# Moving the norm factors' small matmuls and the scaling and convolution of the first results into the third unit's time

## The chip, the cores and the metric

The kernel runs on one core of a Trainium2 chip. The metric is the device time of one execution in microseconds (us). A profile adds the core's span from its first to its last instruction, which is a little shorter. TensorE (PE in the rows) does the matmuls, VectorE (DVE) and ScalarE (ACT) the elementwise work, GpSimd (POOL) a few tiny operations, and SyncE's queue (SP) issues nearly all DMAs.

## The reference

One layer of an encoder over a prompt of 1024 rows and a sample of 256 rows, of width 1024, in float32. What matters here is its first part:

```python
h = rms_norm(x, norms[i, 0])            # x * rsqrt(mean(x*x) + eps) * g
b, c, v = jnp.split(h @ w_in, 3, -1)    # w_in: 1024 x 3072
u = c * v
conv = sum(up[:, j:j+S] * conv_w[j] for j in range(3))   # up: u padded by a row at each end
mix = (b * conv) @ w_out
x = x + rms_norm(mix, norms[i, 1])
```

A gated feed-forward network of width 2816 with its own norms follows.

## The kernel before, in words

**Products.** A float32 product is made of three products of parts: each operand is split into a high part (ScalarE's copy in a rounded type) and a low part (VectorE's subtraction), and `product` (L209) issues high x high, high x low and low x high for each 128 rows of the sum. The prompt's 1024 rows and 1024 features are cut in quarters `a11`, `a12`, `a21`, `a22`, and sums of quarters `s1` to `s4` save one of eight block products (a Strassen-like scheme): one unit of 256 output features takes seven prompt products of 12 matmuls with 512 columns, and two sample products of 24 matmuls with 256 columns. `Block` (L219) holds a unit's PSUM banks `x`, `y`, `z`, `sg`, `su`; its products go x(a11), y(a12), x(s2), z(s1), x(s3), the two sample products, x(a22), z(s4). Between them `x` is copied out by ScalarE, and VectorE adds `y` or `z` to the copy. `make` (L186) splits a unit's weights and forms their sums; `load` (L171) asks for a unit's weights with two DMAs.

**Units.** The 1024 features of each of c, v and b are done in four slices, in the order c, v, b of each slice (`SEQ`). `start` (L516) writes out the first three units by hand, without a scheduler (`manual_schedule`, L720): its order in the code is the order on each engine. The first unit is c, plain products with tiles `c__`, `csg`, `csu`; the second is v (`b = Block(uv, ...)`, PSUM tiles `xv`, `yv`, `zv`, `sgv`, `suv`); the third is b (`b3 = Block(ub, ...)`, L682, tiles `xp__676`, `yp__677`, `zp__678`, `sgp`, `sup`). From the fourth on (L746) a scheduler orders the same steps.

**The norm.** The products are made of x times g alone; the factor 1/rms of each row is applied afterwards, squared, to c times v (`rows_c.end()`, L685 multiplies c's results `row` by `r2`; then `u` = `row` times v). For it, ten row blocks of x are loaded (`load_row`, L476), squared and summed by ScalarE into `rt` (`square_row`, L480). Two of them are in flight; each square frees the place that the next load waits for. `norm_of` (L487) turns four (or two) sums into factors: VectorE's scaling (L122), GpSimd's power (L123), VectorE's square into `rq`, and a split in `rh` (ScalarE) and `rl` (VectorE). `spread` (L497) brings them to all partitions with eight (or four) small matmuls against an identity (`bc`, L503), and ScalarE squares that into `r2` (L508, L510). There are three groups: rows 0 to 3, rows 4 to 7, and the sample's 8 and 9.

**The order around the change.** In the second unit the small matmuls stand before x(s2) (L650), before x(s3) (L666) and before z(s4) (L676). In the third unit VectorE scales, multiplies and convolves (`conv`, L414) c and v after x(a11) (L685 to L700), and the fourth unit's weights are made; the load of the fifth unit's weights (`load(SEQ[4])`, L707) stands before the stores of the first result (`store`, L428, DMAs `zd<-zst`).

Of the kernel before, what the change touches and what calls it, by code (L numbers as in the profile page):

```python
# [14 lines left out]
P = 128  # L15
# [21 lines left out]
def encoder_kernel(ctx: ExitStack, tc: tile.TileContext, xT, x, g0T, gB, cwT, w1, w2, w3, w4, out_p, out_s):  # L37
# [148 lines left out]
    def make(u, what):  # L186

        if u is None:
            return
        rw = raw[u]  # L190
        if what == "sums":
            sub(rw[:, 0], rw[:, 1], rw[:, 0])
            sub(rw[:, 1], rw[:, 2], rw[:, 1])
            sub(rw[:, 2], rw[:, 0], rw[:, 2])
            add(rw[:, 3], rw[:, 3], rw[:, 2])
            return
        blocks = {"g": slice(0, 4, 3), "u": slice(1, 3), "t13": slice(0, 2), "t24": slice(2, 4)}[what]
# [125 lines left out]
    class EvC:  # L323
# [33 lines left out]
    class EvMul:  # L357
# [27 lines left out]
        def add12(self, z):  # L385
            add(self.t["12"], self.t["12"], z)
            self.times(1, 0, self.t["12"])

        def read22(self, x, z, mult=True):
            copy(self.tmp("22"), x)  # L390
            add(self.t["22"], self.t["22"], z)
            if mult:
                self.times(1, 1, self.t["22"])

# [92 lines left out]
    def norm_of(c):  # L487

        t0, n = CH[c]
        i0, m = t0 // P, n // P  # L490
        rc = rt[:, i0 : i0 + m]
        rstd(rc, rc, m)
        mul(rq[:, i0 : i0 + m], rc, rc)
        norms[c] = [small(m, f"r{p}{c}", F32R) for p in "hl"]
        split(*norms[c], rc)
# [20 lines left out]
    def start():  # L516
# [85 lines left out]
        def scaled_add(out, src, f0, other, op=ALU.add):  # L602
            for k in range(KH):
                nc.vector.scalar_tensor_tensor(
                    out=out[:, k], in0=src[:, k], scalar=g0k(f0 + k), in1=other[:, k], op0=ALU.mult, op1=op
                )
# [26 lines left out]
        make(uv, "sums")  # L633
        b.run("x", "g", 0, "a11", True)
        b.run("y", "g", 1, "a12", True)
        make(uv, "t24")
        parts("s1", s1)
        put(s1)
        make(uv, "t13")
        ev.read11(b.bank["x"])  # L640
        ev.add11(b.bank["y"], mult=False)
        for i in range(2, 6):
            square_row(i)
            load_row(i + 2)
            if i == 3:
                norm_of(0)
        b.sample(evac=False)
        scaled_add(s3, xq["a22"], KH, s2)
        parts("s3", s3)
        spread(0, 5)  # L650
        b.run("x", "t24", 0, "s2", False)
        scaled_add(s4, xq["a12"], KH, s2)
        put(s2, s3)
        square_row(6)
        load_row(8)
        ev.read12(b.bank["x"])
        square_row(7)
        load_row(9)
        load(SEQ[3])
        parts("s4", s4)  # L660
        put(s4)
        b.run("z", "t13", 0, "s1", True)
        make(ub, "g")
        make(ub, "u")
        norm_of(1)
        spread(1, 6)  # L666
        b.run("x", "t13", 1, "s3", False)
        b.drop("t13")
        ev.read22(b.bank["x"], b.bank["z"], mult=False)
        for i in (8, 9):  # L670
            square_row(i)
        make(ub, "sums")
        norm_of(2)
        b.run("x", "t24", 1, "a22", False)
        b.drop("t24")
        spread(2, 7)  # L676
        make(ub, "t24")
        b.run("z", "u", 1, "s4", False)
        b.release_u()
        make(ub, "t13")  # L680
        ev3, un = EvMul(0, 0), SEQ[3]
        b3 = Block(ub, ev3)  # L682
        b3.run("x", "g", 0, "a11", True)
        ev3.read11(b3.bank["x"])
        rows_c.end()  # L685
        new_u(0)
        ev.times(0, 0, ev.t["11"])
        ev.times(0, 1, b.bank["x"])
        ev.times(1, 1, ev.t["22"])
        ev.sample(b.bank["sg"], b.bank["su"])  # L690
        ev.add12(b.bank["z"])
        b3.run("y", "g", 1, "a12", True)
        ev3.add11(b3.bank["y"], mult=False)
        make(un, "g")
        b3.run("x", "t24", 0, "s2", False)
        ev3.read12(b3.bank["x"])
        ev.conv(0)
        b3.run("z", "t13", 0, "s1", True)
        make(un, "u")
        ev.end()  # L700
        b3.run("x", "t13", 1, "s3", False)
        b3.drop("t13")
        ev3.times(0, 0, ev3.t["11"])
        make(un, "sums")
        ev3.read22(b3.bank["x"], b3.bank["z"])
        b3.sample(evac=False)
        load(SEQ[4])  # L707
        make(un, "t24")
        ev3.sample(b3.bank["sg"], b3.bank["su"])
        b3.run("x", "t24", 1, "a22", False)  # L710
        b3.drop("t24")
        make(un, "t13")
        ev3.read21(b3.bank["x"])
        b3.run("z", "u", 1, "s4", False)
        b3.release_u()
        ev3.add12(b3.bank["z"])
        ev3.end()

    turn[0] = 6
    with tc.manual_schedule():  # L720
        start()


    w2t, w2r = [], []
# [21 lines left out]
    for n in range(3, len(SEQ)):  # L746
        u = SEQ[n]
        follow = SEQ[n + 1 : n + 3] + [None, None]
        final = n == len(SEQ) - 1
        ev = EvC(u[2]) if u[1] == 1 else EvMul(u[1], u[2])  # L750
        if final:
            put(r2)
            w2_steps()
        b = Block(u, ev, *follow[:2], final)
        b.p12()
        b.p657()
        b.sample()
        if final:
            for i in ORDER2[:2]:
                load_z(i, 0, KD - 2)  # L760
        b.p43()
# [186 lines left out]
    class EvF:  # L948
# [33 lines left out]
        def copy22(self, x):  # L982
            self.c22 = self.tmp("c22")
            copy(self.c22, x)
# [610 lines left out]
```

## Time and profile before

| | us |
|---|---|
| median of 3 runs | 1273.38 (1272.29 to 1276.47) |
| the profiled execution | 1275.11 |
| its span | 1273.3 |
| TensorE busy | 1243.2 |
| VectorE busy | 835.0 |
| ScalarE busy | 464.7 |
| GpSimd busy | 24.0 |
| DMA, mean rate over the span | 163 GB/s |

Every engine works through its own instructions in order and waits at each for what it needs. "Busy" is the time in which instructions of the engine ran; TensorE's weight loads run beside its matmuls. A row of a timeline says when an instruction started, how long it took, the engine, the line, what it wrote and read, and in brackets how long the engine had been idle before it and what ended that. Times are counted from the span's start.

### The profile page before, as it was taken

The page shows a single profiled execution, that of the slowest core. Times are in us where ns is not written, and L with a number is a line of the kernel's source. Part 1 is how long each engine was busy: PE and PEld are TensorE (multiplying, and loading weights), DVE is VectorE, ACT ScalarE, POOL GpSimd, SP SyncE. Part 2 cuts the span into 40 slices and gives each one's busy share as a digit, 9 for nine tenths or more (in the row PEclk, how much of TensorE's full clock was granted, in tenths as well). Part 3 has the DMA queues.
Part 4 walks back from the last instruction along what each step waited for, and adds up shares of the span by engine and source line. Part 5 has one row for each costly group of instructions (what it writes and reads, how often), then busy time and mean ns, then how long its engine had stood idle before and what let it go on. Part 6 is the DMA issues. An engine that isn't in the chain of part 4 may idle for free.

```text
span 1273.3 us, 15950 instructions
## 1 busy us (share of the span) xinstructions
PE 1243.2 (98%) x6239; PEld 1057.2 (83%) x6239; DVE 835.0 (66%) x1157; ACT 464.7 (36%) x695; POOL 24.0 (2%) x49
## 2 busy tenths in 40 slices
PE   9699999999999989999999999999999999999997
PEld 7578888888878878888888888888888888888886
DVE  6857674666376587664755655655647479869566
ACT  7633332334143454343433433433434342212011
POOL 0000000000011100000000000000000000000000
PEclk9889999999999999999999999999999999999999
DMA  8403131233954303542532533524525888766794
GB/s 307 156 1 116 66 115 36 76 116 113 333 194 158 137 34 102 163 151 94 178 121 93 189 114 118 188 88 147 157 88 190 293 282 306 266 229 214 274 337 177
DMA packets 186124, 207.38 MB, mean 163 GB/s; under 512 B 8000, under 2 KB 146368, under 8 KB 185024
## 3 DMA queue, kind: packets, MB, share of 16 engines
q1 hardware_dynamic: 185616, 205.83, 48.3%
q8 instruction: 49, 0.80, 0.3%
q10 hardware_dynamic: 432, 0.53, 0.1%
q14 instruction: 27, 0.22, 0.0%
HBM read 134.89 MB, written 71.43 MB: 162 GB/s over the span
## 4 chain that ended last, share of the span: by engine, by line
PE 87%; DVE 4%; DMA 4%; ACT 3%; issue 1%; POOL 0%; SPq 0%; DVEq 0%; ACTq 0%; POOLq 0%
PE xo L1394 12%; PE zo L1394 6%; PE mx L810 5%; PE yo L1394 3%; DMA wrf__3033<-w 1%; PE xf__3501 L213 1%; PE xp__676 L213 1%; PE xf__3503 L213 1%; PE xf__4757 L213 1%; PE xf__4370 L213 1%; PE xf__7079 L213 1%; PE xf__6866 L213 1%; PE xf__6692 L213 1%; PE xf__6479 L213 1%; PE xf__6305 L213 1%
## 5 line engine op out<-in xcount | busy, mean ns | idle before, releaser
L810 PE MATMUL mx<-w2s,zs 128*128 128x512 f32 x480 | 111.2, 391 | 0.0
L810 PEld LDWEIGHTS mx<-w2s,zs 128*128 128x128 f32 x480 | 89.5, 188 | 18.2
L106 ACT ACTIVATE st<-act 128x640 fp32r<-128x640 f32 x77 | 56.8, 737 | 94.7 <-DMA actd<-st 64.0
L97 DVE TENSOR_TENSOR st<-act,st 128x640 fp32r<-128x640 f32 x77 | 63.2, 820 | 20.9 <-ACT st L106 20.4
L100 DVE TENSOR_TENSOR y<-y,xo 128x512 f32<-128x512 f32 x85 | 58.2, 685 | 27.4 <-PE xo L1394 27.1
L1394 PE MATMUL xo<-w4t,us 128*128 128x512 f32 x273 | 68.9, 389 | 0.0
L1394 PEld LDWEIGHTS xo<-w4t,us 128*128 128x128 f32 x273 | 51.3, 188 | 10.6
L1394 PE MATMUL xo<-w4t,ut 128*128 128x512 f32 x222 | 55.5, 390 | 0.0
L106 ACT ACTIVATE w4t<-w4r 128x1024 fp32r<-128x1024 f32 (+1 forms) x23 | 23.5, 1023 | 72.5 <-DVE w4r L97 59.6
L1394 PEld LDWEIGHTS xo<-w4t,ut 128*128 128x128 f32 x222 | 41.7, 188 | 8.7
L100 DVE TENSOR_TENSOR y<-y,zo 128x512 f32<-128x512 f32 x45 | 30.8, 685 | 17.3 <-PE zo L1394 17.0
L1394 PE MATMUL xo<-w4b,ut 128*128 128x512 f32 x165 | 41.6, 390 | 0.0
L1394 PE MATMUL zo<-w4t,ut 128*128 128x512 f32 x165 | 41.5, 389 | 0.0
L1394 PE MATMUL zo<-w4b,ut 128*128 128x512 f32 x165 | 41.5, 389 | 0.0
L1426 ACT ACTIVATE junk<-y 128x1024 f32<-128x1024 f32 (+1 forms) x12 | 11.0, 919 | 73.7 <-DVE y L100 72.4
L1394 PEld LDWEIGHTS xo<-w4b,ut 128*128 128x128 f32 x165 | 31.0, 188 | 6.6
L1394 PEld LDWEIGHTS zo<-w4t,ut 128*128 128x128 f32 x165 | 31.0, 188 | 6.5
L1394 PEld LDWEIGHTS zo<-w4b,ut 128*128 128x128 f32 x165 | 31.0, 188 | 6.4
L424 DVE SCALAR_TENSOR_TENSOR row<-u,cw,row 128x1024 f32<-128x1024 f32 (+1 forms) x32 | 27.7, 881 | 5.8 <-ACT row L422 5.6
L1394 PE MATMUL yo<-w4b,us 128*128 128x512 f32 x114 | 28.9, 389 | 0.0
L106 ACT ACTIVATE w4b<-w4r 128x512 fp32r<-128x512 f32 (+1 forms) x22 | 18.1, 839 | 28.3 <-DMA us<-actd 12.5
L97 DVE TENSOR_TENSOR w4t<-w4r,w4t 128x1024 fp32r<-128x1024 f32 (+1 forms) x23 | 26.9, 1172 | 0.8 <-ACT w4t L106 0.8
(2115 smaller groups left out, 3357.9 us busy)
## 6 DMA issues: line engine op xcount, KB each, us to landing
actd<-st SPq DMA_DIRECT2D x154, 320.0 KB, 2.9
ut<-actd SPq DMA_DIRECT2D x20, 1024.0 KB, 6.8
us<-actd SPq DMA_DIRECT2D x62, 256.0 KB, 5.0
ut<-actd SPq DMA_DIRECT2D x16, 768.0 KB, 8.8
zd<-zst SPq DMA_DIRECT2D x32, 320.0 KB, 3.1
zs<-zd SPq DMA_DIRECT2D x8, 1024.0 KB, 6.8
w4r<-w SPq DMA_DIRECT2D x11, 512.0 KB, 4.4
w4r<-w SPq DMA_DIRECT2D x22, 256.0 KB, 5.5
```

What stands on the lines that cost most here:

```text
L97: nc.vector.tensor_tensor(out=out, in0=a, in1=b, op=ALU.subtract)
L100: return nc.vector.tensor_tensor(out=out, in0=a, in1=b, op=ALU.add)
L106: nc.scalar.activation(out, a, AF.Copy)
L213: nc.tensor.matmul(out[:, :n], stat(w, k), mov(part, k), start=first and k == 0 and j == 0, stop=last and k == KH - 1 and j == 2, skip_gro ...
L424: nc.vector.scalar_tensor_tensor(out=out, in0=src, scalar=cw[:, j, dd : dd + 1], in1=out, op0=ALU.mult, op1=ALU.add)
L810: nc.tensor.matmul(mx[i][h], zs[i][:, part, k], w2t[k][:, w, h * H : (h + 1) * H], start=k == 0 and j == 0, stop=k == KD - 1 and j == 2,)
L1394: nc.tensor.matmul(acc, stat[n, c, j][:, ap], w[wp], start=starts and jn == 0 and m == 0, stop=jn == len(grp) - 1 and m == 2, skip_group_c ...
L1426: nc.scalar.activation(junk, src, AF.Square, accum_out=acc[:, col : col + 1])
```

## The change

`norm_of` is cut in two: the scaling and power stay, and the square and split become `parts_of_norm`. `read22` becomes `copy22` and `add22`. In `start`, the sums `s3` and `s4` are formed earlier, the squares of rows stand behind the copies of product results, the first group of small matmuls goes behind x(s2), the second and third into the third unit, and what the third unit does on VectorE is reordered. The third unit's PSUM banks are named one by one, and the fourth unit does its sample products earlier. The diff, without the helper lines:

```diff
         make(uv, "t24")
         parts("s1", s1)
         put(s1)
+        scaled_add(s3, xq["a22"], KH, s2)
         make(uv, "t13")
         ev.read11(b.bank["x"])
-        ev.add11(b.bank["y"], mult=False)
-        for i in range(2, 6):
-            square_row(i)
-            load_row(i + 2)
-            if i == 3:
-                norm_of(0)
+        next_row(2)
+        next_row(3)
+        norm_of(0)
         b.sample(evac=False)
-        scaled_add(s3, xq["a22"], KH, s2)
-        parts("s3", s3)
-        spread(0, 5)
-        b.run("x", "t24", 0, "s2", False)
+        high3, low3 = hi_lo("s3", s3)
+        high3(0)
+        high3(2)
+        low3()
         scaled_add(s4, xq["a12"], KH, s2)
         put(s2, s3)
-        square_row(6)
-        load_row(8)
+        next_row(4)
+        next_row(5)
+        parts_of_norm(0)
+        b.run("x", "t24", 0, "s2", False)
         ev.read12(b.bank["x"])
-        square_row(7)
-        load_row(9)
-        load(SEQ[3])
+        ev.add11(b.bank["y"], mult=False)
         parts("s4", s4)
         put(s4)
+        spread(0, 5)
         b.run("z", "t13", 0, "s1", True)
         make(ub, "g")
         make(ub, "u")
-        norm_of(1)
-        spread(1, 6)
         b.run("x", "t13", 1, "s3", False)
         b.drop("t13")
+        make(ub, "sums")
         ev.read22(b.bank["x"], b.bank["z"], mult=False)
-        for i in (8, 9):
-            square_row(i)
-        make(ub, "sums")
-        norm_of(2)
+        next_row(6)
+        next_row(7)
+        load(SEQ[3])
+        norm_of(1)
         b.run("x", "t24", 1, "a22", False)
         b.drop("t24")
-        spread(2, 7)
         make(ub, "t24")
+        parts_of_norm(1)
+        make(ub, "t13")
         b.run("z", "u", 1, "s4", False)
         b.release_u()
-        make(ub, "t13")
...
         b3.run("x", "g", 0, "a11", True)
         ev3.read11(b3.bank["x"])
+        square_row(8)
+        square_row(9)
+        norm_of(2)
+        make(un, "g")
+        b3.run("y", "g", 1, "a12", True)
+        ev3.add11(b3.bank["y"], mult=False)
+        spread(1, 1)
+        parts_of_norm(2)
+        b3.run("x", "t24", 0, "s2", False)
+        ev3.read12(b3.bank["x"])
+        spread(2, 5)
         rows_c.end()
...
+        b3.run("z", "t13", 0, "s1", True)
         ev.times(1, 1, ev.t["22"])
...
+        mul(samp(rows[0]), samp(rows[0]), by_halves(b3.bank["sg"]))
         ev3.read21(b3.bank["x"])
+        make(un, "sums")
+        ev3.add22(b3.bank["z"])
+        make(un, "t24")
         b3.run("z", "u", 1, "s4", False)
         b3.release_u()
...
         ev3.end()
+        make(un, "t13")
+        load(SEQ[4])
...
-        b.p657()
-        b.sample()
+        if n == 3:
+            b.nxt2 = None
+            b.sample()
+            b.p657()
+            load(follow[1])
+        else:
+            b.p657()
+            b.sample()
```

How this moves instructions, at three places. The first is ScalarE's list in the second unit, from the first two squares of rows that the norm's first group needs (`rows_392`, `rows_395`) on; `rh_466` and `rh_533` are the high parts of the first group's factors, before:

```order
L482 ACTIVATE rows_392,rt<-rows_392 128x1024
L482 ACTIVATE rows_395,rt<-rows_395 128x1024
L93 ACTIVATE rh_466<-rt 128x4
L482 ACTIVATE rows_458,rt<-rows_458 128x1024
L482 ACTIVATE rows_461,rt<-rows_461 128x1024
L106 ACTIVATE s3h<-xa_120 128x1024 x2
L508 ACTIVATE r_111<-bc_534 128x512
```

And on ScalarE at the same place after the change:

```order
L488 ACTIVATE rows_392,rt<-rows_392 128x1024
L488 ACTIVATE rows_395,rt<-rows_395 128x1024
L106 ACTIVATE s3h<-xa_120 128x1024 x2
L488 ACTIVATE rows_461,rt<-rows_461 128x1024
L488 ACTIVATE rows_464,rt<-rows_464 128x1024
L93 ACTIVATE rh_533<-rt 128x4
L106 ACTIVATE c__549<-xv__409 128x512
L106 ACTIVATE s4h<-xa_118 128x1024 x2
L519 ACTIVATE r_111<-bc_558 128x512
```

The copies of `s3` moved ahead, and the squares of rows 4 and 5 (`rows_461`, `rows_464`) now stand before the factors' high part.

VectorE's list at the same place, before (`rl_` is the factors' low part, `xa_120` becomes `s3`, `xa_118` becomes `s4`):

```order
L97 TENSOR_TENSOR s1l<-xa_119,s1h 128x1024 x2
L94 TENSOR_TENSOR wt13p__451<-wrp__144,wt13p__451 128x1024
L100 TENSOR_TENSOR c__454<-c__454,yv__410 128x512
L122 TENSOR_SCALAR rt<-rt 128x4
L103 TENSOR_TENSOR rq<-rt 128x4
L94 TENSOR_TENSOR rl_467<-rt,rh_466 128x4
L604 SCALAR_TENSOR_TENSOR xa_120<-xa_120,g_94,xa_117 128x512 x4
L97 TENSOR_TENSOR s3l<-xa_120,s3h 128x1024 x2
L604 SCALAR_TENSOR_TENSOR xa_118<-xa_118,g_94,xa_117 128x512 x4
```

VectorE's list there after the change:

```order
L97 TENSOR_TENSOR s1l<-xa_119,s1h 128x1024 x2
L615 SCALAR_TENSOR_TENSOR xa_120<-xa_120,g_94,xa_117 128x512 x4
L94 TENSOR_TENSOR wt13p__455<-wrp__144,wt13p__455 128x1024
L122 TENSOR_SCALAR rt<-rt 128x4
L97 TENSOR_TENSOR s3l<-xa_120,s3h 128x1024 x2
L615 SCALAR_TENSOR_TENSOR xa_118<-xa_118,g_94,xa_117 128x512 x4
L103 TENSOR_TENSOR rq<-rt 128x4
L94 TENSOR_TENSOR rl_534<-rt,rh_533 128x4
L100 TENSOR_TENSOR c__458<-c__458,yv__410 128x512
```

The forming and splitting of `s3` and the forming of `s4` now stand between the scaling of the sums (L122) and the factors' low part.

The second place is ScalarE's list around the second and the third group, before (`rh_598` and `rh_636` are the high parts of their factors, `bc_602` and `bc_652` what their small matmuls write, `c__624` the copy of x(s3), `wgp__589` to `wt13p__673` the third unit's weights):

```order
L93 ACTIVATE wup__592<-wrp__152 128x1024
L93 ACTIVATE rh_598<-rt 128x4
L508 ACTIVATE r_111<-bc_602 128x512
L106 ACTIVATE c__624<-xv__409 128x512
L482 ACTIVATE rows_561,rt<-rows_561 128x1024
L482 ACTIVATE rows_566,rt<-rows_566 128x1024
L93 ACTIVATE rh_636<-rt 128x2
L510 ACTIVATE r_111<-bc_652 128x2x128
L93 ACTIVATE wt24p__658<-wrp__152 128x1024
L93 ACTIVATE wt13p__673<-wrp__152 128x1024
```

ScalarE's list there after the change (`c__602` is the copy of x(s3), `c__665` and `c__714` are the third unit's first two copies, `wgp__671` is a fourth unit's weight):

```order
L106 ACTIVATE c__602<-xv__409 128x512
L488 ACTIVATE rows_527,rt<-rows_527 128x1024
L488 ACTIVATE rows_530,rt<-rows_530 128x1024
L93 ACTIVATE wt24p__628<-wrp__152 128x1024
L93 ACTIVATE rh_632<-rt 128x4
L93 ACTIVATE wt13p__636<-wrp__152 128x1024
L106 ACTIVATE c__665<-xb__651 128x512
L488 ACTIVATE rows_606,rt<-rows_606 128x1024
L488 ACTIVATE rows_609,rt<-rows_609 128x1024
L93 ACTIVATE wgp__671<-wrp__611 128x1024
L519 ACTIVATE r_111<-bc_687 128x512
L93 ACTIVATE rh_698<-rt 128x2
```

The copy of x(s3), which x(a22) waits for, now stands ahead of the second group, and the third group came behind the third unit's first copy. On TensorE the second group's small matmuls stand behind the third unit's y(a12) and the third group's behind its x(s2).

The third place is SyncE's queue in the third unit, before (`wrp__568` and `wrp__840` are the weights of the fourth and fifth unit, `zd<-zst` the stores of the first result):

```order
L478 DMA rows_566<-x 128x1024
L182 DMA wrp__568<-w 128x2x512
L184 DMA wrp__568<-w 128x1024
L182 DMA wrp__840<-w 128x2x512
L184 DMA wrp__840<-w 128x1024
L434 DMA zd<-zst_864 128x5x128 x2
L434 DMA zd<-zst_869 128x5x128 x2
L434 DMA zd<-zst_888 128x5x128 x2
L434 DMA zd<-zst_893 128x5x128 x2
```

SyncE's queue there after the change (`wrp__611` and `wrp__895` are the same two units' weights):

```order
L484 DMA rows_609<-x 128x1024
L182 DMA wrp__611<-w 128x2x512
L184 DMA wrp__611<-w 128x1024
L440 DMA zd<-zst_848 128x5x128 x2
L440 DMA zd<-zst_853 128x5x128 x2
L440 DMA zd<-zst_882 128x5x128 x2
L440 DMA zd<-zst_887 128x5x128 x2
L182 DMA wrp__895<-w 128x2x512
L184 DMA wrp__895<-w 128x1024
```

The fifth unit's weights moved behind the eight stores. From the fifth unit's first products on, each engine's list is as before.

## Rows read from the trace of the kernel before

**Rows 1.** Waits of TensorE: who waited for whom; total us, times, longest us.

```profile
PE bc L503 <- ACT rh L93: 13.4, 3, 9.9
```

**Rows 2.** Timeline of TensorE, 45 to 96 us: start us, us, what, idle before.

```profile
45.65 0.28 PE L213 MATMUL suv__412<-hsh,wup__386 128*128 128x256 f32 x1
47.86 0.33 PE L503 MATMUL bc<-ident_r,rh 128*128 128x128 f32 x1 [1.93 <-ACT rh L93]
...
48.89 0.45 PE L213 MATMUL xv__409<-s2h,wt24p__442 128*128 128x512 f32 x1
...
64.41 0.48 PE L503 MATMUL bc<-ident_r,rh 128*128 128x128 f32 x1 [9.85 <-ACT rh L93]
...
66.18 0.73 PE L213 MATMUL xv__409<-s3h,wt13p__451 128*128 128x512 f32 x1
...
72.04 0.50 PE L213 MATMUL xv__409<-a22h,wt24p__442 128*128 128x512 f32 x1 [0.69 <-ACT c__624 L106]
...
76.63 0.33 PE L503 MATMUL bc<-ident_r,rh 128*128 128x128 f32 x1 [1.59 <-ACT rh L93]
...
95.25 0.28 PE L213 MATMUL sgp__679<-hsh,wgp__589 128*128 128x256 f32 x1
```

**Rows 3.** Stretches: us, busy of each engine, granted clock, DMA share, GB/s.

```profile
57.26:70.91 13.65, 6.50 (x19) 5.51 (x20) 5.91 (x9) 4.69 (x6) 1.02 (x1) 0.50 0.41 149
77.74:81.15 3.41, 3.41 (x10) 2.64 (x9) 2.38 (x3) 1.95 (x3) 0.00 (x0) 0.50 0.00 0
```

**Rows 4.** The chain that ended last, 66 to 88 us: start us, us, what.

```profile
66.39 4.99 PE xv__409 L213 x12
...
77.38 4.39 PE zv__413 L213 x12
...
84.53 2.72 PE yp__677 L213 x12
```

**Rows 5.** Timeline of ScalarE, 45 to 52 us.

```profile
45.12 1.04 ACT L482 ACTIVATE rows<-rows 128x1024 f32<-128x1024 f32 x1
...
48.86 1.06 ACT L482 ACTIVATE rows<-rows 128x1024 f32<-128x1024 f32 x1 [1.05 <-DMA rows<-x]
...
50.91 1.06 ACT L482 ACTIVATE rows<-rows 128x1024 f32<-128x1024 f32 x1 [0.90 <-DMA rows<-x]
```

**Rows 6.** Timeline of VectorE, 42 to 104 us.

```profile
42.03 2.35 DVE L97 TENSOR_TENSOR s1l<-xa,s1h 128x1024 fp32r<-128x1024 f32 x2
44.30 1.22 DVE L94 TENSOR_TENSOR wt13p__451<-wrp__144,wt13p__451 128x1024 fp32r<-128x1024 f32 x1
...
47.92 2.73 DVE L604 SCALAR_TENSOR_TENSOR xa<-xa,g,xa 128x512 f32<-128x512 f32 x4
...
81.05 2.88 DVE L103 TENSOR_TENSOR row<-row,r 128x1280 f32<-128x1280 f32 x2
...
91.67 3.27 DVE L424 SCALAR_TENSOR_TENSOR row<-u,cw,row 128x1024 f32<-128x1024 f32 x4 [2.09 <-ACT row L422]
...
102.56 0.68 DVE L100 TENSOR_TENSOR c__788<-c__788,zp__678 128x512 f32<-128x512 f32 x1
```

**Rows 7.** Timeline of GpSimd: its power operations.

```profile
46.54 1.03 POOL L123 TENSOR_TENSOR rt<-rt,nhalf 128x4 f32<-128x4 f32 x1 [45.24 <-DVE rt L122]
...
455.17 0.54 POOL L123 TENSOR_TENSOR n_8t<-n_8t,nhalf 128x1 f32<-128x1 f32 x1 [0.62 <-DVE n_8t L122]
462.88 1.45 POOL L123 TENSOR_TENSOR n_9t<-n_9t,nhalf 128x1 f32<-128x1 f32 x1 [7.17 <-DVE n_9t L122]
```

**Rows 8.** DMA issues: what, queue, count, KB each, median us to landing.

```profile
wrp__144<-w SPq DMA_DIRECT2D x2, 512.0 KB, 10.5
wrp__568<-w SPq DMA_DIRECT2D x2, 512.0 KB, 6.0
wrp__840<-w SPq DMA_DIRECT2D x2, 512.0 KB, 4.3
```

**Rows 9.** Timeline of VectorE, 462.6 to 463 us.

```profile
462.72 1.22 DVE L97 TENSOR_TENSOR a22l<-ar,a22h 128x1024 fp32r<-128x1024 f32 x1
```

More of the change, by code (lines that the diff above doesn't have):

```diff
@@ L387, in add12, with copy22, add22 @@
             self.times(1, 0, self.t["12"])
+        def copy22(self, x):
+            copy(self.tmp("22"), x)
+        def add22(self, z):
+            add(self.t["22"], self.t["22"], z)
         def read22(self, x, z, mult=True):
-            copy(self.tmp("22"), x)
-            add(self.t["22"], self.t["22"], z)
+            self.copy22(x)
+            self.add22(z)
             if mult:
@@ L492, in norm_of, with parts_of_norm @@
         rstd(rc, rc, m)
+    def parts_of_norm(c):
+        t0, n = CH[c]
+        i0, m = t0 // P, n // P
+        rc = rt[:, i0 : i0 + m]
         mul(rq[:, i0 : i0 + m], rc, rc)
@@ L635, in start, with hi_lo, high, low @@
         b.run("y", "g", 1, "a12", True)
+        def hi_lo(name, src):
+            hi, lo = new_c(name)
+            def high(k):
+                copy(hi[:, k : k + 2], src[:, k : k + 2])
+            def low():
+                for k in (0, 2):
+                    sub(lo[:, k : k + 2], src[:, k : k + 2], f32(hi[:, k : k + 2]))
+            return high, low
+        def next_row(i):
+            square_row(i)
+            if i + 2 < NT:
+                load_row(i + 2)
         make(uv, "t24")
@@ L664, in start @@
         make(ub, "u")
-        norm_of(1)
-        spread(1, 6)
         b.run("x", "t13", 1, "s3", False)
         b.drop("t13")
+        make(ub, "sums")
         ev.read22(b.bank["x"], b.bank["z"], mult=False)
-        for i in (8, 9):
-            square_row(i)
-        make(ub, "sums")
-        norm_of(2)
+        next_row(6)
+        next_row(7)
+        load(SEQ[3])
+        norm_of(1)
         b.run("x", "t24", 1, "a22", False)
         b.drop("t24")
-        spread(2, 7)
         make(ub, "t24")
+        parts_of_norm(1)
+        make(ub, "t13")
         b.run("z", "u", 1, "s4", False)
         b.release_u()
-        make(ub, "t13")
         ev3, un = EvMul(0, 0), SEQ[3]
-        b3 = Block(ub, ev3)
+        b3 = Block(ub, ev3, banks={q: new_ps(f"{q}b_", n) for q, n in (("x", 6), ("y", 7))})
         b3.run("x", "g", 0, "a11", True)
         ev3.read11(b3.bank["x"])
+        square_row(8)
[9 more added lines that the diff above has]
+        spread(2, 5)
         rows_c.end()
@@ L688, in start @@
         ev.times(0, 1, b.bank["x"])
+        ev.sample(b.bank["sg"], b.bank["su"])
+        b3.bank.update({q: new_ps(f"{q}b_", n) for q, n in (("z", 7), ("sg", 1), ("su", 5))})
+        b3.run("z", "t13", 0, "s1", True)
         ev.times(1, 1, ev.t["22"])
-        ev.sample(b.bank["sg"], b.bank["su"])
         ev.add12(b.bank["z"])
[L692 to L696, printed above, removed]
         ev.conv(0)
-        b3.run("z", "t13", 0, "s1", True)
-        make(un, "u")
-        ev.end()
         b3.run("x", "t13", 1, "s3", False)
@@ L703, in start @@
         ev3.times(0, 0, ev3.t["11"])
-        make(un, "sums")
-        ev3.read22(b3.bank["x"], b3.bank["z"])
+        ev3.copy22(b3.bank["x"])
+        ev.end()
+        make(un, "u")
         b3.sample(evac=False)
-        load(SEQ[4])
-        make(un, "t24")
-        ev3.sample(b3.bank["sg"], b3.bank["su"])
         b3.run("x", "t24", 1, "a22", False)
         b3.drop("t24")
-        make(un, "t13")
+        mul(samp(rows[0]), samp(rows[0]), by_halves(b3.bank["sg"]))
         ev3.read21(b3.bank["x"])
+        make(un, "sums")
+        ev3.add22(b3.bank["z"])
+        make(un, "t24")
         b3.run("z", "u", 1, "s4", False)
         b3.release_u()
+        mul(samp(rows[1]), samp(rows[1]), by_halves(b3.bank["su"]))
+        ev3.times(1, 1, ev3.t["22"])
         ev3.add12(b3.bank["z"])
         ev3.end()
-    turn[0] = 6
+        make(un, "t13")
+        load(SEQ[4])
     with tc.manual_schedule():
         start()
+    turn[0] = 3
     w2t, w2r = [], []
```

## The prediction

> **What bounds the kernel now.** I read the table of busy times first: TensorE runs 1243.2 of 1273.3 us, so what the other engines do matters only where TensorE waits. The list of waits comes next: its largest entry by far is the small matmuls `bc`, 13.4 us in three waits on ScalarE's `rh` [rows 1]. The timeline of TensorE shows where they lie: pauses of 1.93, 9.85 and 1.59 us before the three groups, and one of 0.69 us before x(a22), 14.06 us in all, between the end of the second unit's sample products and the third unit's [rows 2]. The stretches then show a second loss: TensorE's clock was granted at half, 1.2 instead of 2.4 GHz, from 57.26 to 70.91 us, from inside the long pause to 6.5 us after it, and again from 77.74 to 81.15 us, soon after the pause of 1.59 us [rows 3]. A product of 12 matmuls takes 2.72 us at the full clock, and 4.99 and 4.39 us in these two stretches [rows 4].
>
> The whole loss of this stage: from 45.77 us (the last sample matmul starts at 45.65 and hands on 0.12 us later, as half of what a 512-column matmul takes, 2.72 / 12) to 95.25 us are 49.48 us [rows 2, 4]. In it stand ten products of 2.72 us, 27.20, and the small matmuls: a group of eight takes 48.89 - 47.86 = 1.03 us at the full clock, so two groups of eight and one of four are 2.6 us. 49.48 - 29.8 = 19.7 us lost. The printed pauses are 14.1 of it; the other 5.6 are the low clock (2.27 us in x(s3), 1.67 in z(s4), and 66.18 - 64.41 - 1.03 = 0.74 in a group of eight, 4.7 together) and the drain of the matmul ahead of each pause, which the pauses leave out.
>
> **The change part by part.** It adds and removes no matmul, no DMA and no large elementwise operation; all is order. So I walk each engine through its new list with the old durations.
>
> *First group, now behind x(s2).* TensorE reaches x(s2) at 45.77 us and is through at 48.49. It then needs `rh` and `rl`. ScalarE's list is unchanged up to the square of row 3, which starts at 45.12 and ends with its read of the sum near 46.3 [rows 5]. Then it copies `s3` (2 us), and waits for row 4, whose load waits for the same square as before and so should land as before: the squares of rows 4 and 5 start at 48.86 and 50.91 us, both behind a DMA [rows 5]. `rh` stands behind the second, so it starts near 52.0 and the first small matmul at 52.2. VectorE ends the split of `s1` at 42.03 + 2.35 = 44.38 us. Then come `s3` (2.73), the low part of `wt13p` (1.2), the scaling of the sums (0.1), the split of `s3` (two halves, 2.3 as for `s1`) and `s4` (2.7), so 53.3 us; then the factors' square and `rl`, 53.5 us [rows 6]. The second small matmul starts there, and the group ends at 53.5 + 7/8 of 1.03 = 54.4 instead of 48.49 + 1.03 = 49.5: 4.9 us lost, one pause of 3.7 and one of 1.2 us. Before, this group's pause was 1.93; the change makes it longer. VectorE's list sets it, and ScalarE's is 1.3 us behind that.
>
> *Second and third group, now in the third unit.* x(s3) follows z(s1) at once, and the copy out of `x` is no longer behind a group, so the pauses of 9.85 and 1.59 us go. The same wait of x(a22) for that copy stays, since the three stand in the same order: 0.7 us and the drain, 0.85. What is late next: counted at the full clock, the copy of x(s3) ends near 60.5 us; two squares (2.1), scaling, power (1.03, [rows 7]) and splits give `rl` at 65; TensorE comes to the second group only after z(s4), x(a11) and y(a12), at 71.4. The third group's squares stand behind the copy of the third unit's x(a11) (69.5 us), a weight's split stands between, and `rl` comes at 74.5; TensorE arrives at 75.0. That is 0.5 us of room, and I cost it at nothing.
>
> *Scaling and convolution.* VectorE's list from the first scaling to the addition of z took 103.24 - 81.05 = 22.2 us with a pause of 2.09 us in it [rows 6]. Now z(s4) of the third unit waits for that addition (`add22` stands late). In the new list I find 1.2 us of a weight split gone, some 2 us of products and store splits more, and the pause for ScalarE's `conv` shorter: again about 22. TensorE needs, from the third group to z(s4), five products and three sample products (as many columns): 8 x 2.72 = 21.8 us. A tie; I take 0.2 us, with 0 and 1.5 as bounds.
>
> *Weight loads.* The fifth unit's load stands behind the eight stores. By the same walk the last store's split ends 6.5 us before TensorE wants this weight's high part; the issue (0.5), a landing of 4.3 us [rows 8] and ScalarE's copy (1 us) leave 1.0 us or less. The sixth unit's copy of a weight stands on ScalarE ahead of the copy that frees `x`; its room is about as small. I cost both at nothing, and price a late landing below.
>
> *The clock.* The trace has no pause of 4.9 us. Nearest below is that of 1.93 us, behind which x(s2) ran at the full clock and lost nothing; nearest above is that of 9.85, which cost 2.27 + 0.74 = 3.0 us [rows 2, 4]. The pause of 1.59 us, close behind another, cost 1.67. I take the middle of the two costly ones, 2.4 us, with 0 and 4.7 (both together) as bounds, because TensorE does next to nothing in this pause.
>
> *Sum.* Lost before 19.7; after 4.9 + 0.85 + 0.2 + 2.4 = 8.35. Gain 11.3 us. The lists agree from the fifth unit's first products on, and the later waits hang on TensorE's own progress, so I expect the gain to come through whole. The profiled execution took 1275.11 us (its span 1273.3 and 1.8 around it): 1263.8. The median of the three runs is 1.73 us lower, so 1262.1.
>
> A rule that speaks against this: before, VectorE stood still during the first power, since it waited for it. Now that power runs beside VectorE's split of `s3`. A power of one column takes 0.54 us alone and took 1.45 where a subtraction of 128x1024 began 0.16 us before it [rows 7, 9]: it was held, and came through after one such instruction. The Trainium skill (SBUF — State Buffer, "SBUF: two separate sides") says why: GpSimd and a VectorE operation with two inputs in SBUF contend for one pair of ports, an exclusive lock, and the loser blocks fully. By the trace the power ends near 51 us, ahead of 52.0, and costs nothing; what it costs if it isn't let in between VectorE's instructions is the second rival.
>
> **The rivals.**
> 1. The clock stays at its full level: 2.4 us less, 1259.7. For it: the pause of 1.93 us cost nothing. Against it: this one is 2.5 times as long.
> 2. The power is held until VectorE itself stops for its result, at 53.3 us: plus 1.03 us of power, the square, `rh` and `rl`, and TensorE goes on 1.3 us later, 1263.4. Against it: 1.45 us beside VectorE, not more [rows 7].
> 3. Slower than before: the two weight loads land late. Where TensorE waits for a landing of L us, each load costs L less 4.3 and its room of 1.0, and a pause of some us costs clock too, up to 4.7 us for both. The gain is gone when 2 (L - 5.3) + 4.7 = 11.3, at L = 8.6. At 6.0 us, as the load beside the row blocks took, it costs 1.4: 1263.5. At 10.5 us, as in the crowded start, it costs 10.4 + 4.7: 1277 [rows 8]. Against it: at this point of the program little else than the stores runs, and the load there took 4.3.
> 4. The change doesn't do what it says: the small matmuls still wait in the third unit, since squares and powers come late there too. Each us that `rl` of the third group comes late beyond 0.5 costs one; with 3 us late, and the clock for it, 1266.
>
> **How the numbers follow.** The forecast 0.58 (its own range 1260.5 to 1264), rival 1 0.17, rival 2 0.06, rival 3 0.10, of which 0.03 at or above 1273, and rival 4 0.09. The range reaches from the full clock, with 1 us for the spread of the runs, to rival 4 with the same: 1258.5 to 1267. A measurement here can tell about 0.3%, 3.8 us, from no change. Faster by more than that, below 1269.6: 0.92; within: 0.05; slower: 0.03.
>
> **What would show it right or wrong.** Right: the list of waits has one or two entries of `bc`, some 5 us together, on `rh` and then on `rl` (VectorE), all near 48 to 54 us; no `bc` wait in the third unit; one stretch of half clock behind 50 us and none near 77; the third unit's first sample matmul near 84 us instead of 95.25. Wrong in its main step: a pause at the second or third group, or waits of the fourth and fifth unit's matmuls on `wgp` or on `add22` of more than 1 us.

## The result: 10.4 us faster, and the profile after

The changed kernel took 1263.19 us (median of 5 runs, 1262.17 to 1263.55) against 1273.61 us, a ratio of 0.9911 (95% interval 0.9897 to 0.9926). The profiled execution took 1262.17 us, its span 1260.4. The forecast was 1262.1 us. The means of the five runs each differ by 11.3 us, close to the 11.4 by which the stage below is shorter.

The list of waits of TensorE, total us, times, longest us. It answers to [rows 1]:

```profile
PE bc L514 <- ACT rh L93: 3.5, 1, 3.5
PE bc L514 <- DVE rl L94: 1.2, 1, 1.2
PE xv__409 L213 <- ACT c__602 L106: 0.7, 1, 0.7
```

13.4 us on `rh` have become 3.5, and 1.2 us on VectorE's `rl` are new. The timeline of TensorE, which answers to [rows 2]:

```profile
44.91 0.40 PE L213 MATMUL xv__409<-s2h,wt24p__442 128*128 128x512 f32 x1
...
51.32 0.48 PE L514 MATMUL bc<-ident_r,rh 128*128 128x128 f32 x1 [3.50 <-ACT rh L93]
52.99 0.47 PE L514 MATMUL bc<-ident_r,rl 128*128 128x128 f32 x1 [1.20 <-DVE rl L94]
...
62.49 0.50 PE L213 MATMUL xv__409<-a22h,wt24p__442 128*128 128x512 f32 x1 [0.69 <-ACT c__602 L106]
...
73.50 0.22 PE L514 MATMUL bc<-ident_r,rh 128*128 128x128 f32 x1
...
77.12 0.22 PE L514 MATMUL bc<-ident_r,rh 128*128 128x128 f32 x1
77.18 0.27 PE L514 MATMUL bc<-ident_r,rl 128*128 128x128 f32 x1
...
83.02 0.28 PE L213 MATMUL sgb__739<-hsh,wgp__580 128*128 128x256 f32 x1
...
99.89 0.50 PE L213 MATMUL zb__738<-s4h,wup__583 128*128 128x512 f32 x1
```

All pauses are now in the first group and at x(a22). The second group (73.50) and the third (77.12) carry no wait. The stage from x(s2) to the third unit's first sample matmul takes 83.02 - 44.91 = 38.11 us; before it took 49.48 [rows 2]. With the same 29.8 us of work in it, the loss has gone from 19.7 to 8.3 us. I measure every kernel below by this length too: it leaves out the spread of the rest of the program, but it is taken from one execution of each.

Stretches with the granted clock (the figure right behind the busy times of the five engines: 0.50), answering to [rows 3], and the chain behind the pause, answering to [rows 4]:

```profile
51.03:57.85 6.82, 5.33 (x16) 4.47 (x17) 6.27 (x10) 5.18 (x7) 0.00 (x1) 0.50 0.43 149
```

```profile
54.75 4.31 PE zv__413 L213 x12
...
65.50 2.72 PE zv__413 L213 x12
```

One stretch at 1.2 GHz is left of two, and z(s1) pays for it: 4.31 us for twelve matmuls that take 2.72 at 2.4 GHz.

Who makes the first group late is read on the other engines. ScalarE's timeline [rows 5], GpSimd's [rows 7] and VectorE's [rows 6]:

```profile
48.49 1.06 ACT L488 ACTIVATE rows<-rows 128x1024 f32<-128x1024 f32 x1 [0.70 <-DMA rows<-x]
...
49.73 1.06 ACT L488 ACTIVATE rows<-rows 128x1024 f32<-128x1024 f32 x1
...
51.07 0.20 ACT L93 ACTIVATE rh<-rt 128x4 fp32r<-128x4 f32 x1 [0.18 <-POOL rt L123]
```

```profile
47.97 3.06 POOL L123 TENSOR_TENSOR rt<-rt,nhalf 128x4 f32<-128x4 f32 x1 [46.66 <-DVE rt L122]
```

```profile
47.79 2.35 DVE L97 TENSOR_TENSOR s3l<-xa,s3h 128x1024 fp32r<-128x1024 f32 x2
50.07 2.73 DVE L615 SCALAR_TENSOR_TENSOR xa<-xa,g,xa 128x512 f32<-128x512 f32 x4
...
52.79 0.15 DVE L94 TENSOR_TENSOR rl<-rt,rh 128x4 fp32r<-128x4 f32 x1
...
76.45 0.15 DVE L94 TENSOR_TENSOR rl<-rt,rh 128x2 fp32r<-128x2 f32 x1
...
99.16 0.68 DVE L100 TENSOR_TENSOR c__775<-c__775,zb__738 128x512 f32<-128x512 f32 x1
```

`rh` waits for the power, which took 3.06 us instead of 1.03 and ended, at 51.03, only 0.96 us after VectorE was through with the two subtractions of `s3l` (50.07); `rl` stands behind `s3` and `s4` on VectorE. The third group's `rl` is done at 76.60, 0.6 us before its matmul. `add22` ends at 99.84, and z(s4) starts at 99.89: the tie that was forecast.

### The profile page after: what moved, and what is told of

It is laid out like the page before. It is cut to its first block, busy times and chain, and to the rows that moved or that the text cites. A ratio compares the mean times of both kernels' runs of the same rounds, so it can differ in the third digit from the quotient of the medians.

```text
span 1260.4 us, 15942 instructions
## 1 busy us (share of the span) xinstructions
PE 1240.4 (98%) x6239; PEld 1055.7 (84%) x6239; DVE 835.0 (66%) x1157; ACT 464.9 (37%) x695; POOL 26.2 (2%) x49
## 4 chain that ended last, share of the span: by engine, by line
PE 91%; DVE 4%; DMA 2%; ACT 2%; issue 1%; POOL 0%; SPq 0%; POOLq 0%; DVEq 0%; ACTq 0%
PE xo L1438 12%; PE mx L854 7%; PE zo L1438 6%; PE yo L1438 3%; PE xf__3501 L213 1%; PE xp__1068 L213 1%; PE xb__651 L213 1%; PE xf__3503 L213 1%; PE xf__4931 L213 1%; PE xf__7253 L213 1%; PE xf__7079 L213 1%; PE xf__6866 L213 1%; PE xf__6692 L213 1%; PE xf__6479 L213 1%; PE xf__6305 L213 1%; PE xf__6092 L213 1%
```

## The experiments

Three theories are tried. Theory L: the lists of VectorE and ScalarE set the second unit, and the small matmuls only show where TensorE meets them. Theory P: the place of the small matmuls is the cost. Theory C: the half clock comes from the pause ahead of it. The table has each kernel's time, its ratio to the kernel before (95% interval) and the stage's length:

| kernel | us | ratio | stage, us |
|---|---|---|---|
| changed | 1263.19 | 0.9911 (0.9897 to 0.9926) | 38.11 |
| all groups late | 1261.67 | 0.9906 (0.9890 to 0.9921) | 36.51 |
| before, two groups moved | 1265.85 | 0.9939 (0.9926 to 0.9951) | 41.32 |
| lists reordered | 1256.82 | 0.9869 (0.9855 to 0.9884) | 30.46 |
| filler in the pause | 1260.95 | 0.9897 (0.9883 to 0.9910) | 35.64 |
| first group early | 1264.94 | 0.9920 (0.9904 to 0.9936) | 38.47 |
| second group back | 1269.36 | 0.9963 (0.9949 to 0.9978) | 43.33 |
| fourth unit as before | 1263.64 | 0.9913 (0.9898 to 0.9928) | 37.09 |
| s4 ahead of s3's low part | 1263.05 (one run) | | 38.05 |
| lists reordered, first group early | 1259.47 | 0.9884 (0.9868 to 0.9901) | 32.72 |
| lists reordered, first group in a gap | 1255.36 | 0.9854 (0.9838 to 0.9870) | 30.09 |
| second group back, scaling first | 1263.89 | 0.9925 (0.9912 to 0.9939) | 38.52 |

**All groups late.**

```diff
         put(s4)
-        spread(0, 5)
...
+        spread(0, 5)
         spread(1, 1)
```

> The eight small matmuls of the first group are moved behind the third unit's y(a12), ahead of the second group; nothing else changes. Theory P (the place of the small matmuls is what costs): the pauses of 3.5 and 1.2 us and the half clock behind them (z(s1) 4.31 us instead of 2.72) go and nothing takes their place: 1263.2 - 4.7 - 1.6 = 1256.9 us. Theory L (the lists of ScalarE and VectorE set this stretch; a waiting small matmul only shows it): TensorE runs into waits it does not have now, at x(s3) for the copy of x(s2), which stands behind the square of row 5 (about 1.5 us), at x(a22) for the copy of x(s3), which stands behind two weight copies (about 1.6), and at z(s4) for VectorE's add22, which stands behind a unit's low parts and sums (about 2.6): 5.6 us of pauses against 5.4 now. Only the clock comes back, at most: 1261 to 1263 us, and no bc entry in the list of waits.

1261.67 us: theory L. The timeline of TensorE shows three pauses, the first and the last of them new and the one at x(a22) twice as long, 4.5 us together against 5.4:

```profile
51.75 0.50 PE L213 MATMUL xv__409<-s3h,wt13p__455 128*128 128x512 f32 x1 [0.89 <-ACT c__549 L106]
...
56.26 0.50 PE L213 MATMUL xv__409<-a22h,wt24p__442 128*128 128x512 f32 x1 [1.45 <-ACT c__592 L106]
...
61.45 0.50 PE L213 MATMUL zv__413<-s4h,wup__386 128*128 128x512 f32 x1 [2.18 <-DVE c__592 L100]
```

Not even the clock came back: z(s4), behind the longest of them, took 4.61 us.

**The kernel before, with the second and third group moved alone.**

```diff
-        spread(1, 6)
...
-        spread(2, 7)
...
         ev3.read11(b3.bank["x"])
+        b3.run("y", "g", 1, "a12", True)
+        ev3.add11(b3.bank["y"], mult=False)
+        spread(1, 1)
+        spread(2, 5)
```

The lines of y(a12) move up with them; their old place further down, and the naming of the PSUM banks that this needs, are left out here.

> The kernel before, with one part of the change alone: the small matmuls of the second and third group stand in the third unit (behind y(a12)), with the banks that this needs; squares, copies, splits and scaling keep their order of before. Theory P: the pauses of 9.85 and 1.59 us go with the clock behind them, as in the whole change, and the first group keeps its short pause of 1.93: 1273.6 - 11.4 - 4.7 + 2 (x(a22)'s wait, a little clock) = 1259 to 1262 us. Theory L: the copy of x(s3) still stands behind the squares of rows 6 and 7, which wait for their loads, so x(s3) waits about 1.8 us and x(a22) about 7 us for ScalarE's copy; of 14.1 us of pauses some 10 stay, with a stretch of half clock: 1269 to 1270 us.

1265.85 us, between the two: the place alone brings 7.5 of the 10.4 us. How the rest divides between the new order of squares and sums and the scaling and convolution in the third unit, no run tells. One pause is left beside the first group's, and the cause that I had expected for it was wrong. TensorE, ScalarE and VectorE:

```profile
64.68 0.80 PE L213 MATMUL xv__409<-a22h,wt24p__442 128*128 128x512 f32 x1 [5.88 <-ACT c__614 L106]
```

```profile
63.94 0.20 ACT L93 ACTIVATE rh<-rt 128x4 fp32r<-128x4 f32 x1 [2.54 <-POOL rt L123]
64.05 0.58 ACT L106 ACTIVATE c__614<-xv__409 128x512 f32<-128x512 f32 x1
```

```profile
60.23 1.22 DVE L94 TENSOR_TENSOR wgp__589<-wrp__152,wgp__589 128x1024 fp32r<-128x1024 f32 x1
61.44 1.22 DVE L94 TENSOR_TENSOR wup__592<-wrp__152,wup__592 128x1024 fp32r<-128x1024 f32 x1
62.58 0.16 DVE L122 TENSOR_SCALAR rt<-rt 128x4 f32<-128x4 f32 x1
```

The copy that x(a22) needs stands behind the second group's `rh`, not behind a square; `rh` waits for the power, and the power for VectorE's scaling, which stands behind two weight splits.

**All groups late, and the lists reordered.**

```diff
         next_row(4)
-        next_row(5)
-        parts_of_norm(0)
         b.run("x", "t24", 0, "s2", False)
         ev.read12(b.bank["x"])
-        ev.add11(b.bank["y"], mult=False)
+        next_row(5)
         parts("s4", s4)
         put(s4)
-        spread(0, 5)
         b.run("z", "t13", 0, "s1", True)
-        make(ub, "g")
-        make(ub, "u")
         b.run("x", "t13", 1, "s3", False)
         b.drop("t13")
-        make(ub, "sums")
         ev.read22(b.bank["x"], b.bank["z"], mult=False)
+        parts_of_norm(0)
+        ev.add11(b.bank["y"], mult=False)
+        make(ub, "g")
+        make(ub, "u")
+        make(ub, "sums")
...
+        spread(0, 5)
         spread(1, 1)
```

> All three groups late as in the run with all groups late, and besides the lists of the second unit reordered so that what TensorE needs stands first: ScalarE copies x(s2) before the square of row 5 and x(s3) before the two weight copies, VectorE adds z (add22) before the first group's parts, add11 and the low parts and sums of the next unit. No operation is added. Theory L: one pause of about 1 us is left (x(a22) for the copy of x(s3)), the clock stays full in the second unit, and the third unit's z(s4) still meets VectorE's list within 0.2 us: 4.7 us of lists and 1.6 us of clock less than the changed kernel, 1256 to 1257.5 us. Theory P: no better than the run with all groups late. If a third limit stands right behind (the third group's squares, the scaling and convolution on VectorE), 1259 to 1261.

1256.82 us, as theory L had it. One pause is left in the stage, and further on one for the fifth unit's weights (waits of TensorE):

```profile
PE xv__409 L213 <- ACT c__576 L106: 0.7, 1, 0.7
PE xp__1068 L213 <- ACT wgp__932 L93: 0.6, 1, 0.6
```

**Filler in the pause.**

```diff
         put(s4)
+        fill = new_ps("fill", 7)
+        for k in range(14):
+            nc.tensor.matmul(fill, b.W("t24", 0)(0, k % 4), b.C("s2")(0, k % 4), start=k == 0, stop=k == 13)
         spread(0, 5)
```

> The changed kernel, with 14 more matmuls of 512 columns into a spare bank between x(s2) and the first group of small matmuls (about 3.2 us of work in the pause of 3.5 us; the result of them is not used). Theory C (the half clock from 51.03 to 57.85 us comes from the pause and costs 1.6 us in z(s1)): no stretch of half clock there, z(s1) 2.72 us, the first small matmul at the same time as now, 1261.5 us. Rival (the half clock has nothing to do with the pause): half clock as now, 1263.2 us. If the matmuls of z(s1) run full and the time stays at 1263.2, VectorE's list, not TensorE, sets the end of this stretch.

1260.95 us, with no half clock in the stage. Counted from x(s2) (45.88 us here, 44.91 in the changed kernel), `rh` and `rl` come as late as without it, within 0.2 us, but TensorE, and the chain behind it, go on at 2.4 GHz:

```profile
52.13 0.33 PE L514 MATMUL bc<-ident_r,rh 128*128 128x128 f32 x1 [0.17 <-ACT rh L93]
53.81 0.33 PE L514 MATMUL bc<-ident_r,rl 128*128 128x128 f32 x1 [1.35 <-DVE rl L94]
```

```profile
54.80 2.79 PE zv__413 L213 x12
```

From `rl`'s matmul to z(s1) 0.99 us instead of 1.76, and 1.52 less in z(s1): 2.3 us for the clock. The stage is 2.5 us shorter and the time 2.2 (the intervals of the two ratios overlap; the traces tell them apart).

**First group early.**

```diff
-        scaled_add(s3, xq["a22"], KH, s2)
...
         norm_of(0)
+        parts_of_norm(0)
         b.sample(evac=False)
+        spread(0, 5)
+        scaled_add(s3, xq["a22"], KH, s2)
...
-        parts_of_norm(0)
...
-        spread(0, 5)
```

> The changed kernel with the first group alone put back to where it was: its splits behind the power, its small matmuls ahead of x(s2), and s3 formed behind them on VectorE as before. Theory P: the pause there is 1.9 us again instead of 4.7, and the clock stays up: 2.8 + 2.3 us less, 1258 us. Theory L: what the first group no longer holds up meets the lists further on, as with all groups late: x(a22) waits about 2.1 us for the copy of x(s3) and z(s4) about 2.5 for add22, and the clock may fall behind these; stage as long as in the changed kernel within 1.5 us: 1262 to 1264.5 us.

1264.94 us, 0.4 above the range of theory L; the intervals of the two ratios overlap, so the changed kernel is no better or worse than this by more than they can tell: theory L. The group's own pause is 2.10 us, and 2.03 come back at z(s4), which waits for `add22`; x(a22) waits 0.69 us as in the changed kernel, where 2.1 were expected, and the clock falls behind both pauses:

```profile
47.56 0.33 PE L514 MATMUL bc<-ident_r,rh 128*128 128x128 f32 x1 [2.10 <-ACT rh L93]
...
64.36 0.50 PE L213 MATMUL zv__413<-s4h,wup__386 128*128 128x512 f32 x1 [2.03 <-DVE c__602 L100]
```

**Second group back.** The lines taken out where the changed kernel has them are left out here.

```diff
+        next_row(6)
+        next_row(7)
+        load(SEQ[3])
         make(ub, "g")
         make(ub, "u")
+        norm_of(1)
+        parts_of_norm(1)
+        spread(1, 1)
         b.run("x", "t13", 1, "s3", False)
```

> The changed kernel with the second group alone put back: squares of rows 6 and 7, power and splits ahead of x(s3), the eight small matmuls between z(s1) and x(s3) as before. The first group stays behind x(s2) and the third in the third unit. Theory P and L both: a pause of about 6 us at that group, for rh behind the squares and their loads, 5 to 7 us more than the changed kernel and a second stretch of half clock (1.7 to 3 us, as in the kernel before): 1269.5 to 1273 us. Rival (the gain came from squares and copies, not from this group's place): within 2 us of 1263.

1269.36 us, 0.1 below what was expected, but the pause is 3.76 us and not 6, and its cause is another: the squares are done at 57.18, and the scaling follows the two weight splits at 60.44. TensorE, then VectorE:

```profile
62.06 0.33 PE L514 MATMUL bc<-ident_r,rh 128*128 128x128 f32 x1 [3.76 <-ACT rh L93]
```

```profile
59.30 1.22 DVE L94 TENSOR_TENSOR wup__592<-wrp__152,wup__592 128x1024 fp32r<-128x1024 f32 x1
60.44 0.16 DVE L122 TENSOR_SCALAR rt<-rt 128x4 f32<-128x4 f32 x1
```

**Second group back, with its scaling first.** Against the kernel above:

```diff
         load(SEQ[3])
-        make(ub, "g")
-        make(ub, "u")
         norm_of(1)
         parts_of_norm(1)
+        make(ub, "g")
+        make(ub, "u")
         spread(1, 1)
```

> The kernel with the second group put back, with one further move: the group's scaling, power and splits stand ahead of the next unit's two weight splits (g and u) instead of behind them; the eight small matmuls stay between z(s1) and x(s3). In the kernel with the second group back, the squares of rows 6 and 7 are done at 57.08 us, but VectorE scales the sums only at 60.44, behind the low parts of g and u, and rh follows the power at 61.80. Theory L (the wait called rh is VectorE's list): scaling near 57.2, power 1.0, rh near 58.5, where TensorE arrives at 58.3; the pause of 3.8 us and the half clock behind it (x(s3) 4.41 us) go: 1269.4 - 3.5 - 1.7 = 1264.2 us, so that this group costs little more in the second unit than in the third. Theory P (a group in the second unit costs its place): 1268 to 1270 us, another wait in place of this one.

1263.89 us, and an interval that overlaps the changed kernel's. The same group, still between z(s1) and x(s3), no longer waits at all, and x(s3) runs at full clock (VectorE, TensorE, the chain):

```profile
57.50 0.17 DVE L122 TENSOR_SCALAR rt<-rt 128x4 f32<-128x4 f32 x1 [1.69 <-ACT rows L488]
```

```profile
59.06 0.33 PE L514 MATMUL bc<-ident_r,rh 128*128 128x128 f32 x1
```

```profile
60.25 2.81 PE xv__409 L213 x12
```

So 5.5 us of the time (4.8 of the stage) were in the order of work on VectorE, GpSimd and ScalarE, with the small matmuls left where they had been.

**The fourth unit's order of before.**

```diff
-        if n == 3:
-            b.nxt2 = None
-            b.sample()
-            b.p657()
-            load(follow[1])
-        else:
-            b.p657()
-            b.sample()
+        b.p657()
+        b.sample()
```

> The changed kernel with the fourth unit's products in the order of before (p657, then the sample products, no late load). The prediction costed this part and the weight loads around it at nothing: 1263.2 us, within 1 us. Rival (this order is worth something because the fifth unit's load stands behind the stores and lands late): a wait of the fourth or fifth unit's matmuls on a weight copy of 1 us or more, 1264.5 us or above.

1263.64 us: no difference that can be measured, and no wait on a weight among TensorE's waits.

**s4 ahead of s3's low part.**

```diff
-        low3()
         scaled_add(s4, xq["a12"], KH, s2)
+        low3()
```

> The changed kernel, but VectorE forms s4 ahead of the low part of s3, so that the first power (GpSimd) runs beside VectorE's four scalar_tensor_tensor instructions (128x512, 2.73 us) instead of its two tensor_tensor subtractions (128x1024, 2.35 us). In the changed kernel the power takes 3.06 us, 0.9 beyond the end of the subtractions. If any two-input VectorE instruction holds it: 3.3 to 3.8 us. If only the subtractions do and it runs beside the others: 1.0 to 1.3 us, and rh waits for the square of row 5 alone (start about 50.9 us). The time stays within 1 us of 1263 either way, since rl waits for VectorE's list.

GpSimd's timeline:

```profile
48.36 1.45 POOL L123 TENSOR_TENSOR rt<-rt,nhalf 128x4 f32<-128x4 f32 x1 [47.06 <-DVE rt L122]
```

VectorE's:

```profile
48.19 1.41 DVE L615 SCALAR_TENSOR_TENSOR xa<-xa,g,xa 128x512 f32<-128x512 f32 x2
```

Neither number: the power took 1.45 us. It ends at 49.81, 0.96 us after the first of the four instructions gives way to the second (at 48.85), as it ended 0.96 us after the second of the two subtractions in the changed kernel. That looks like a power that was held by the first of the four and got in before the second; with one run and one such order it is not shown. The time stayed, since `rl` waits for VectorE's list.

**The reordered lists, with the first group early.** Against the kernel with reordered lists:

```diff
-        scaled_add(s3, xq["a22"], KH, s2)
...
         norm_of(0)
+        parts_of_norm(0)
         b.sample(evac=False)
+        spread(0, 5)
+        scaled_add(s3, xq["a22"], KH, s2)
```

The lines taken out further down are left out, here and in the next diff.

> The kernel with reordered lists, but with the first group alone ahead of x(s2) again (splits behind the power, s3 formed behind them), as in the kernel before. With the lists out of the way nothing behind should swallow what this group loses: its pause of 2.1 us, and the clock behind it if it falls (the same group in the run with the first group early had a half-clock matmul right behind it): 1256.8 + 2 to 4 = 1259 to 1261 us. Rival (the place of a group never matters, some list always sets the end): 1256.8 us, within 1.

1259.47 us. With the lists in order, its pause of 1.93 us and the drain ahead of it are paid in full: 2.3 us of the stage and 2.7 of the time (the intervals of the two ratios overlap).

**The reordered lists, with the first group in a gap.** Against the same kernel:

```diff
+        parts_of_norm(0)
         parts("s4", s4)
...
         norm_of(1)
+        spread(0, 5)
         b.run("x", "t24", 1, "a22", False)
```

> The kernel with reordered lists, with the first group between x(s3) and x(a22) and its splits on VectorE ahead of the split of s4: its eight small matmuls fill the 0.7 us in which x(a22) waits for the copy of x(s3). The pause goes and the stage from x(s2) to the third unit's sample products, 30.46 us, loses 0.4 to 0.8, of which the third group's rl may take some back: 1256 to 1256.8 us, which the spread of the runs hardly tells from 1256.82. Rival (the splits ahead of s4 delay z(s4)): a wait at z(s4), 1257.5 us or above.

1255.36 us. The list of waits has no matmul of this stage; the eight small ones end right before x(a22):

```profile
54.56 0.27 PE L514 MATMUL bc<-ident_r,rl 128*128 128x128 f32 x1
54.88 0.50 PE L213 MATMUL xv__409<-a22h,wt24p__442 128*128 128x512 f32 x1
```

The stage is 30.09 us, 0.3 above its work. This is the fastest kernel here; its interval overlaps that of the one with reordered lists.

## Why the prediction was right, and what it left out

- **The loss that goes.** Forecast 19.7 us lost before and 8.35 after; measured 19.7 and 8.3. The second and third group wait no more, and the later waits did not swallow the gain.
- **The first group.** Forecast pauses of 3.7 and 1.2 us, measured 3.50 and 1.20. The walk along VectorE's list was right for `rl`. For `rh` it was right by chance: I let it wait for the square of row 5, which was to start at 50.91 behind its load, until 52.0. The square started at 49.73 and waited for no load; the power, held until 51.03, set `rh`, 0.2 us after the square's end. In the run with the second group's scaling first, the same load held row 5's square until 50.74 again and `rh` until 51.80.
- **x(a22) and `add22`.** Forecast 0.85 and 0.2; measured 0.87 with the drain (0.69 of it printed), and no wait. The tie was costed with 2.72 us for a sample product; one takes 2.87 (83.02 to 85.89), so TensorE needs about 0.5 us more up to z(s4) than the 21.8 of the forecast.
- **The clock.** Forecast 2.4 us as the middle of two prices, measured 2.3 with the filler. By the same reckoning the runs with the fourth unit as before (1.43 us from `rl`'s matmul to z(s1), and 3.98 in z(s1)) and with s4 first (1.76 and 4.76) paid 1.6 and 2.7 us for pauses of nearly the same length; that the forecast came within 0.1 us is chance. Rival 1 fell: a pause of 3.5 us costs clock. But the price is not a function of the pause: of four pauses of 1.9 to 2.1 us in the first group, two were followed at once by 3.4 us of half clock (before with two groups moved; first group early) and two were not (reordered lists with the group early; the kernel before [rows 2]). The first matmul of x(s2) behind the pause took 0.74 and 0.73 us where the clock had fallen, and 0.45 where it had not (in the order of the first three names; the kernel before also took 0.45):

```profile
49.38 0.74 PE L213 MATMUL xv__409<-s2h,wt24p__442 128*128 128x512 f32 x1
```

```profile
48.96 0.73 PE L213 MATMUL xv__409<-s2h,wt24p__442 128*128 128x512 f32 x1
```

```profile
48.96 0.45 PE L213 MATMUL xv__409<-s2h,wt24p__442 128*128 128x512 f32 x1
```

- **The held power (rival 2).** It was held, though only until the subtractions ended, at 51.03 against the 51 us of the walk, and not until 53.3. That the numbers agree is in part chance: the walk let the power in after one subtraction, and it was held through two, but VectorE came to the scaling at 47.73, 0.6 us ahead of the walk.
- **The weight loads (rival 3).** The room was costed at 1.0 us or less with a landing of 4.3 us [rows 8]. The landing is now 5.3, and no matmul waited; with the lists reordered, where it is 5.8, one waits 0.6 us, and the fourth unit's old order changes nothing. The room was there, and hardly larger. DMA issues:

```profile
wrp__895<-w SPq DMA_DIRECT2D x2, 512.0 KB, 5.3
```

- **Rival 4** fell: no `bc` wait stands in the third unit.
- **What was left out.** The sum treats its terms as if each could be had alone. It prices the first group's move at a loss (a pause of 1.93 us becoming 4.9, and 2.4 of clock); undone, at most 1.5 us come back, which the runs do not tell from nothing, since z(s4) then waits for VectorE's `add22` (first group early), and with the group late x(s3) waits, and x(a22) waits longer, for ScalarE's copies too. And it read the wait of 9.85 us as one on ScalarE's `rh`, to be escaped by moving the small matmuls. Of the 5.2 us of the stage that the second group costs in the second unit of the changed kernel (43.33 against 38.11), 4.8 came from VectorE's scaling standing behind two weight splits. The kernel before had the same order; the last square of the group ended 5.6 us before VectorE's scaling, with the split of `s4` and these two between them:

```profile
57.00 0.19 ACT L482 ACTIVATION_READ_ACCUMULATOR rows<-rows 128x1 f32 x1
```

```profile
60.44 1.22 DVE L94 TENSOR_TENSOR wgp__589<-wrp__152,wgp__589 128x1024 fp32r<-128x1024 f32 x1
61.65 1.22 DVE L94 TENSOR_TENSOR wup__592<-wrp__152,wup__592 128x1024 fp32r<-128x1024 f32 x1
62.79 0.16 DVE L122 TENSOR_SCALAR rt<-rt 128x4 f32<-128x4 f32 x1
```

No run moves that scaling alone in the kernel before, so how much of the 9.85 us it made there is not shown. VectorE's list is the next limit, as its busy time shows: in the changed kernel 13.45 of the 14 us from 44 to 58. The total was right because the whole list was walked; its terms are not what each edit is worth.

## What to carry to other kernels

A wait names the instruction that came last, not the list that made it late: follow it back over every engine (here ScalarE's split, GpSimd's power, VectorE's scaling, and the two weight splits ahead of it), and move the short instruction that starts this chain first. Before moving work on the engine that waits, write down what it would meet next if this wait were gone; moving the first group was worth 1.5 us at most, in the two places tried, until the other engines' lists were put in the order in which TensorE needs them, and then the same stage ran with 0.3 us of loss. Work that fits a short remaining gap (eight small matmuls of 1.0 us before x(a22)) belongs there; that took 0.4 us off the stage, too little for the runs' times to tell.

## What the runs showed of the hardware that was not expected

- GpSimd's power on 128x4 takes 1.02 to 1.03 us alone, 3.06 or 3.07 beside two subtractions of 128x1024 that start 0.18 us ahead of it (in all eight runs that kept this order), and 1.45 beside four `scalar_tensor_tensor` of 128x512 (one run). In both orders it ends 0.96 us after an instruction of VectorE gives way to the next (50.07 to 51.03, 48.85 to 49.81), but it did not get in between the first and the second subtraction. The Trainium skill (SBUF — State Buffer, "SBUF: two separate sides") has the loser of the shared ports blocked for the winner's whole instruction. The trace agrees that the power is blocked, and shows it blocked through VectorE's next instruction as well, 1.2 us more (half of 2.35).
- The half clock after a short pause comes or does not come with the same pause in the same place (above), and lasted 3.4 us in one profiled run with the changed kernel's stage (fourth unit as before, z(s1) 3.98 us) and 6.8 us in another (the changed kernel, 4.31). From the first small matmul to z(s1) the run with two groups moved took 5.47 us with such a stretch (47.71 to 53.18) and the reordered lists with the first group early 3.81 us without (47.93 to 51.74): 1.7 us that one trace has or has not.
